# One wait in the issue order of a hybrid decoder layer: the recurrence's output products are issued two dense blocks behind the products of its states

## The chip, the cores and the metric

The kernel runs on one core of a Trainium2 chip. The metric is the device time of one execution in microseconds (us); before the change it is 469.66 us, the median of three runs (467.76 to 470.64).

## What is computed

One layer of a decoder trunk, for 512 tokens of width 1024, all in fp32. The parts that the change touches are the HGRN2 recurrence and what surrounds it; cut from the reference:

```python
xn = rmsnorm(h, norm_gain[i]).astype(dt)
proj = xn @ w_in[i]
aq, ak, av, ag, bq, bf, bi, bg, gate_a, gate_b = jnp.split(proj, split_pts, axis=-1)
...
def step(state, inp):
    qc, kc, vc, gc = inp
    cum = jnp.cumsum(gc, axis=2)
    o_inter = jnp.einsum('bhtk,bhkv->bhtv', qc * jnp.exp(cum), state)
    diff = jnp.where(causal[:, :, None], cum[:, :, :, None, :] - cum[:, :, None, :, :], LOG_DECAY_MASK)
    scores = jnp.einsum('bhtk,bhsk,bhtsk->bhts', qc, kc, jnp.exp(diff))
    o_intra = jnp.einsum('bhts,bhsv->bhtv', scores, vc)
    last = cum[:, :, -1:, :]
    state = state * jnp.exp(last[:, :, 0, :, None]) + jnp.einsum('bhsk,bhsv->bhkv', kc * jnp.exp(last - cum), vc)
    return state, o_inter + o_intra
...
yb = rmsnorm(yb, hgrn_out_gain[i].reshape(HGRN_HEADS, HGRN_VDIM)).reshape(b, s, HGRN_WIDTH)
yb = (yb * jax.nn.silu(bg.astype(f32))).astype(dt) @ w_up_b[i]
merged = jax.nn.sigmoid(gate_a.astype(f32)) * ya.astype(f32) + jax.nn.sigmoid(gate_b.astype(f32)) * yb.astype(f32)
h = h + merged.astype(dt) @ w_out[i]
```

Beside it stand a block-sparse attention with 8 heads (`ya`) and a last product with a gate (`ple`).

## The kernel before

**Dense blocks.** Every fp32 product with a weight is made of three matmuls of a rounded part and a rest (`hi*hi`, `hi*lo`, `lo*hi`). A block of one projection, 128 output columns by 512 tokens, is 24 such matmuls of 128x512 (`mm3`, L253). Its weight of 512 KB is loaded by GpSimd's queue (L227), rounded on ScalarE (`wh`, L194), and the rest is taken on VectorE (`wl`, L195); `weight` runs these two blocks ahead. The blocks stand in a fixed list, `ORDER`: for each head of the recurrence a forget block `bf` and a query block `bq`, the gates `bg` and `ag`, and the merge gates `ga` and `gb`, whose sigmoid is three instructions on ScalarE (L258 to L260).

**Side work on a planned clock.** Attention and recurrence are Python generators. Every dense matmul advances a planned clock `now` by 0.227 us (a block by 5.45 us), and a generator that yields a number is continued when the planned clock has gone on by so much. So a yielded number says how many dense blocks go in between. TensorE and SyncE keep the order in which the program issues; ScalarE's and VectorE's instructions are put in order by a scheduler that simulates the program. On each engine the order is then fixed.

**The recurrence of one head** (4 heads, h0 to h3; `hop` of h1 stands at 197 us of the profile, that of h2 at 251 us). `hgrn_intra` makes rescaled copies of keys and queries at seven sizes (`hx`, L496 to L504), and multiplies them on TensorE into two PSUM banks, `lpb` and `lpa` (L546, L551, L519): `lpb` and the first part of `lpa` beside one attention step, the rest of `lpa` (sizes 8, 4, 2) beside the next. The results are merged into `s32` (L527) and copied into the scores `sc` (L560, L563, L598). It also transposes the decayed keys through a trip to memory (L577 and four DMAs of L579, on SyncE's queue) and unpacks them on ScalarE (`hkd`, L589). `hgrn_out` multiplies keys and values into `hds` (L606), runs the states `st` through it (L610, L613), yields, and then issues seven matmuls into `hop` (L619, L621) that need `sc` and `st`. Then comes a chain that is narrow and goes to and fro: square on ScalarE (L625), transpose and sums on VectorE (L273, L275), L278 on ScalarE, L280, L264 and L265, L266 to L269, `nwide` on ScalarE (L293), transpose on VectorE (L294), and at last L627, which reads `hop` and scales it into `ho`. `hgrn_gated` multiplies by the gate (L633) and splits the result into `ybh` and `ybl`, which the blocks `ub` need.

**The banks.** `lpb`, `lpa`, `hds` and `hop` are taken in this order from two PSUM banks (tag "g"). So `lpa` of a head lies in the bank of the previous head's `hop`, and its first matmul may not start before L627 has read that `hop`.

**Attention** runs eight steps; each issues score matmuls `s` (L712), a softmax (L729 on VectorE, L731 and L733 on ScalarE) and 16 sorting DMAs on SyncE's queue (L747).

Of the kernel before, what the change touches and what calls it, by code (L numbers as in the profile page):

```python
# [57 lines left out]
def hybrid_layer_kernel(  # L58
# [29 lines left out]
    def unit(tag, name, dt=F32, shape=(128, 512)):  # L88
        return sb.tile(list(shape), dt, tag=tag, bufs=BUFS[tag], name=name)

    def bank(tag, name):
        return psum.tile([128, 512], F32, tag=tag, bufs={"mm": 3, "g": 2, "a": 3}[tag], name=name)
# [34 lines left out]
    def cost(us):  # L127
        now[0] += us
# [142 lines left out]
    def token_sums(sq, tmp, scale):  # L271

        V.transpose(tmp, sq)  # L273
        part = sb.tile([128, 16], F32, tag="n16", bufs=2, name="npart")
        V.tensor_reduce(part, tmp.rearrange("p (j c) -> p j c", c=32), axis=AX.X, op=OP.add)  # L275
        quad = sb.tile([32, 16, 4], F32, tag="n64", bufs=2, name="nquad")
        for i in range(4):
            A.activation(quad[:, :, i], part[32 * i:32 * i + 32], AF.Copy, scale=scale)  # L278
        ms = sb.tile([32, 16], F32, tag="n16", bufs=2, name="nms")
        V.tensor_reduce(ms, quad, axis=AX.X, op=OP.add)  # L280
        return ms

    def token_factor(ms):
        y = sb.tile([32, 16], F32, tag="n16b", bufs=2, name="ny")
        t = sb.tile([32, 16], F32, tag="n16b", bufs=2, name="nt")
        rsqrt(y, t, ms)
        return y

    def token_spread(dst, y):

        wide = sb.tile([128, 16], F32, tag="n16", bufs=2, name="nwide")
        for i in range(4):
            A.activation(wide[32 * i:32 * i + 32], y, AF.Copy)  # L293
        V.transpose(dst, wide[:, :, None].to_broadcast([128, 16, 32]))  # L294
# [306 lines left out]
    def hgrn_out(h, vb):  # L601
        kb, q, cum, kts = hg[h][:4]
        hv = slice(h * 128, h * 128 + 128)
        dsp = bank("g", f"hds{h}")
        for c in range(3):
            PE.matmul(dsp[:, c * 128:c * 128 + 128], kts[:, c * 128:c * 128 + 128], vb[c][:, hv],  # L606
                      start=True, stop=True)
        cost(0.65)
        st = unit("st", f"st{h}", shape=(128, 3, 128))
        V.tensor_copy(st[:, 0], dsp[:, 0:128])  # L610
        for c in (1, 2):
            e = c * 128 + 127
            V.scalar_tensor_tensor(st[:, c], st[:, c - 1], cum[:, e:e + 1], dsp[:, c * 128:c * 128 + 128],  # L613
                                   op0=OP.mult, op1=OP.add)
        yield 6.0
        op_ = bank("g", f"hop{h}")
        for c in range(NT):
            s_ = slice(c * 128, c * 128 + 128)
            PE.matmul(op_[:, s_], vb[c][:, hv], sc[:, c, :], start=True, stop=(c == 0))  # L619
            if c:  # L620
                PE.matmul(op_[:, s_], st[:, c - 1], q[:, s_], start=False, stop=True)  # L621
        cost(1.5)
        o = unit("YB", f"ho{h}")
        y = unit("N", f"hy{h}")
        A.activation(o, op_, AF.Square)  # L625
        token_spread(y, token_factor(token_sums(o, y, 1.0 / 128)))
        V.scalar_tensor_tensor(o, op_, ogain[:, h:h + 1], y, op0=OP.mult, op1=OP.mult)  # L627
        hg[h] += (o,)
# [11 lines left out]
    def hgrn_rest(h, vb, sbg, res):  # L640
        yield from hgrn_out(h, vb)
        yield from hgrn_gated(h, sbg, res)
# [400 lines left out]
```

## Time and profile before

| | us |
|---|---|
| median of three runs (lowest, highest) | 469.66 (467.76, 470.64) |
| the profiled execution | 471.74 |
| its span, first to last instruction | 470.0 |
| TensorE matmul busy | 457.8 |
| VectorE busy | 298.9 |
| ScalarE busy | 277.3 |
| mean granted TensorE clock | 0.984 |

The table of waits names for an engine which instruction it waited for: the total in us, how often, and the longest. A window row gives the busy time of each engine in a stretch, the granted TensorE clock (PEclk, 1.00 is full speed), the busy share of the DMA engines and GB/s. The chain of waits lists start, duration and piece, followed back from the last instruction. A timeline row gives start, duration, engine, line and operation, and in brackets the idle time of its engine just ahead of it and what ended that. Where two instructions follow each other without a gap, the second one's start lies some 0.1 us ahead of the first one's end.

### The profile page before, as it was taken

How to read it: one execution, taken by the hardware profiler on the slowest of the kernel's cores; microseconds unless marked ns; L12 is line 12 of the kernel's file. 1: busy time of each engine (PE TensorE's matmuls, PEld its weight loads, DVE VectorE, ACT ScalarE, POOL GpSimd, SP SyncE). 2: the span in 40 equal slices, each digit the busy share in tenths (PEclk: the TensorE clock that was granted, in tenths of full speed). 3: DMA queues.
4: the chain of work that ended last, by engine and by line, in shares of the span. 5: the costliest groups of instructions: out<-in, count | busy, mean ns of one | idle time of the engine just before them, and what ended most of it. 6: DMA issues, size and time to landing. Idle time of an engine off the chain costs nothing.

```text
span 470.0 us, 8130 instructions
## 1 busy us (share of the span) xinstructions
PE 457.8 (97%) x3094; PEld 378.8 (81%) x3094; DVE 298.9 (64%) x608; ACT 277.3 (59%) x532; POOL 38.4 (8%) x77
## 2 busy tenths in 40 slices
PE   9999999999999999699996999999999999999996
PEld 8888888788888888588885888878888788888886
DVE  5669694867698694958676572654459854553232
ACT  5758575657689886859776784965334522232201
POOL 0000100100000000000100000001111110000000
PEclk9999999999999999889997999999999999999999
DMA  8732333322323633333426153135534544223211
GB/s 249 279 98 91 111 129 107 95 87 78 102 90 93 202 96 118 106 92 130 130 68 166 54 154 117 54 84 168 176 83 133 190 147 144 100 94 111 89 46 45
DMA packets 26470, 55.30 MB, mean 118 GB/s; under 512 B 6720, under 2 KB 12608, under 8 KB 26432
## 3 DMA queue, kind: packets, MB, share of 16 engines
q0 software_dynamic: 9056, 32.51, 21.6%
q1 hardware_dynamic: 17232, 22.27, 15.4%
q8 instruction: 24, 0.39, 0.4%
q14 instruction: 14, 0.11, 0.1%
q10 hardware_dynamic: 144, 0.01, 0.0%
HBM read 46.65 MB, written 2.88 MB: 105 GB/s over the span
## 4 chain that ended last, share of the span: by engine, by line
PE 89%; DVE 4%; ACT 4%; issue 1%; DMA 1%; ACTq 0%; DVEq 0%
PE ga L253 10%; PE gb L253 10%; PE g L253 9%; PE h L253 8%; PE av L383 5%; PE bq L253 5%; PE ub L253 5%; PE bf L253 5%; PE bg L253 4%; PE bi L383 4%; PE aq L383 4%; PE ak L383 4%; PE ua L253 3%; PE pe L253 2%; PE ag L253 2%; PE s L712 2%
## 5 line engine op out<-in xcount | busy, mean ns | idle before, releaser
L194 ACT ACTIVATE wh<-wf 128x1024 fp32r<-128x1024 f32 (+1 forms) x78 | 75.5, 969 | 105.6 <-PE g L253 20.9
L195 DVE TENSOR_TENSOR wl<-wf,wh 128x1024 fp32r<-128x1024 f32 (+1 forms) x78 | 86.5, 1110 | 65.2 <-ACT wh L194 64.6
L227 POOL DMA_DIRECT2D wf<-in_w_tr_dram x30 | 15.8, 528 | 186.2 <-DVE wl L195 128.3
L253 PE MATMUL g<-hh,wh 128*128 128x512 f32 (+1 forms) x72 | 26.3, 365 | 0.0
L253 PE MATMUL g<-hl,wh 128*128 128x512 f32 (+1 forms) x72 | 26.3, 365 | 0.0
L253 PE MATMUL g<-hh,wl 128*128 128x512 f32 (+1 forms) x72 | 26.3, 365 | 0.0
L253 PE MATMUL ga<-xh,wh 128*128 128x512 f32 x64 | 26.0, 405 | 0.0
L253 PE MATMUL gb<-xh,wh 128*128 128x512 f32 x64 | 25.6, 401 | 0.0
L253 PE MATMUL ga<-xh,wl 128*128 128x512 f32 x64 | 25.4, 397 | 0.0
L253 PE MATMUL gb<-xl,wh 128*128 128x512 f32 x64 | 25.4, 397 | 0.0
L253 PE MATMUL ga<-xl,wh 128*128 128x512 f32 x64 | 25.4, 397 | 0.0
L253 PE MATMUL gb<-xh,wl 128*128 128x512 f32 x64 | 25.3, 395 | 0.0
L253 PE MATMUL h<-ml,wh 128*128 128x512 f32 x64 | 25.0, 391 | 0.2 <-DVE ml L195 0.2
L253 PE MATMUL h<-mh,wl 128*128 128x512 f32 x64 | 24.9, 390 | 0.0
L253 PE MATMUL h<-mh,wh 128*128 128x512 f32 x64 | 24.9, 389 | 0.0
L731 ACT ACTIVATE pb<-pb,ps 128x128 f32<-128x128 f32 (+3 forms) x32 | 17.6, 552 | 11.7 <-DVE ps L729 11.7
L729 DVE CUSTOM_DVE_ANT_0 pb<-s,bias 128x128 f32<-128x128 f32 (+3 forms) x28 | 12.7, 494 | 12.6 <-PE s L712 12.6
L930 DVE TENSOR_TENSOR hf<-h,xres 128x512 f32<-128x512 f32 x8 | 5.5, 691 | 18.1 <-PE h L253 18.1
L733 ACT ACTIVATE pb<-pb,ps 128x128 f32<-128x128 f32 (+3 forms) x32 | 15.9, 549 | 0.0
L498 ACT ACTIVATE hx<-hx 128x512 f32<-128x512 f32 x24 | 14.8, 623 | 1.4 <-DVE hx L497 1.3
L253 PEld LDWEIGHTS g<-hh,wl 128*128 128x128 f32 x72 | 13.6, 189 | 2.2
L253 PEld LDWEIGHTS g<-hh,wh 128*128 128x128 f32 x72 | 13.6, 189 | 2.2
(342 smaller groups left out, 1256.1 us busy)
## 6 DMA issues: line engine op xcount, KB each, us to landing
wf<-in_w_tr_dram POOLq DMA_DIRECT2D x30, 512.0 KB, 4.0
wf<-in_w_tok_dram POOLq DMA_DIRECT2D x8, 512.0 KB, 3.7
wf<-in_w_up_dram POOLq DMA_DIRECT2D x16, 256.0 KB, 2.9
wf<-in_w_o_dram POOLq DMA_DIRECT2D x8, 512.0 KB, 3.5
wf<-in_w_g_dram POOLq DMA_DIRECT2D x8, 512.0 KB, 3.6
wf<-in_w_tok_dram SPq DMA_DIRECT2D x6, 512.0 KB, 3.8
pb<-pb SPq DMA_DIRECT2D x64, 48.0 KB, 2.5
bias<-in_ed_dram SPq DMA_DIRECT2D x8, 256.0 KB, 5.4
```

Of the source, the lines that this page charges most:

```text
L194: A.activation(hi, src, AF.Copy)
L195: V.tensor_tensor(lo, src, hi.bitcast(F32), op=OP.subtract)
L227: (G if len(wraw) >= FAR else nc.sync).dma_start(raw, ap)
L253: PE.matmul(ps, a[:, k, :], b[k], start=(n == 0), stop=(n == tot - 1))
L383: PE.matmul(banks[t], a[:, s_], b[:, kk, :], start=(k == 0 and i == 0), stop=(k == KD - 1 and i == 2))
L498: A.activation(x, x, AF.Exp)
L712: PE.matmul(b_[:, o:o + nk], (qh, ql, qh)[i][js, qb * 128:qb * 128 + 128], (kh, kh, kl)[i][js, :nk], start=(i == 0), stop=(i == 2))
L729: in_order(V.tensor_tensor_reduce(p_, s_[:, so:so + nk], T[j][:, nk - 1::-1], -1.0, 3e38, OP.add, OP.min, st[:, 0:1]))
L731: A.activation(p_, p_, AF.Exp, bias=st[:, 0:1], scale=-1.0, accum_out=st[:, 1:2])
L733: A.activation(p_, p_, AF.Copy, scale=st[:, 2:3])
L930: V.tensor_tensor(t, ps, xres, op=OP.add)
```

## The change

One number: the yield in `hgrn_out` between the states' products and the output's.

```diff
@@ -612,7 +612,7 @@
             e = c * 128 + 127
             V.scalar_tensor_tensor(st[:, c], st[:, c - 1], cum[:, e:e + 1], dsp[:, c * 128:c * 128 + 128],
                                    op0=OP.mult, op1=OP.add)
-        yield 6.0
+        yield 11.0
         op_ = bank("g", f"hop{h}")
         for c in range(NT):
             s_ = slice(c * 128, c * 128 + 128)
```

No instruction is added or removed on TensorE. SyncE's order stays as it is, and GpSimd's issues stay in their places. The seven `hop` matmuls of each head go one dense block further back. In h0 they pass part of the `ak` products and a transpose, in h1 the block `gb`, in h2 and h3 a block `ga`.

TensorE in h1, before (`hop` directly behind the last matmul of `ag`):

```order
 L253 MATMUL ag_2106<-xh_487,wl_1858 128x512
-L619 MATMUL hop_2144<-sc,biv_393 128x128
-L619 MATMUL hop_2144<-sc,biv_395 128x128
-L621 MATMUL hop_2144<-ha_1376,st_2088 128x128
-L619 MATMUL hop_2144<-sc,biv_397 128x128
-L621 MATMUL hop_2144<-ha_1376,st_2088 128x128
-L619 MATMUL hop_2144<-sc,biv_399 128x128
-L621 MATMUL hop_2144<-ha_1376,st_2088 128x128
-L253 MATMUL gb_2201<-xh_414,wh_1901 128x512
```

The whole block `gb` stood behind `hop`. In the changed program `hop` follows the last matmul of `gb`:

```order
+L253 MATMUL gb_2155<-xh_487,wl_1902 128x512
+L619 MATMUL hop_2191<-sc,biv_393 128x128
+L619 MATMUL hop_2191<-sc,biv_395 128x128
+L621 MATMUL hop_2191<-ha_1376,st_2088 128x128
+L619 MATMUL hop_2191<-sc,biv_397 128x128
+L621 MATMUL hop_2191<-ha_1376,st_2088 128x128
+L619 MATMUL hop_2191<-sc,biv_399 128x128
+L621 MATMUL hop_2191<-ha_1376,st_2088 128x128
 L253 MATMUL bf_2242<-xh_414,wh_2102 128x512
```

Behind `bf` come three matmuls of `bq`, the scores `s`, `lpb` and `lpa` of the next head, in the same order as before. So one block fewer lies between `hop` and that `lpa`.

ScalarE in h1, at the chain behind `hop` (`nquad`, `nt`, `ny`, `nwide` are the chain; `hkd` the unpacked keys; `wh` rounded weights; `sgb` a sigmoid of `gb`; `ybh` the gated result):

```order
 L278 ACTIVATE nquad<-npart 32x16 x4
 L264 ACTIVATE nt<-nms,epsc 32x16
 L265 ACTIVATE ny<-nt 32x16
+L589 ACTIVATE hkd_2399<-hkt_2403 128x4x3x32
+L194 ACTIVATE wh_2269<-wf_2267 128x1024
 L293 ACTIVATE nwide<-ny 32x16 x4
-L589 ACTIVATE hkd_2399<-hkt_2403 128x4x3x32
-L194 ACTIVATE wh_2238<-wf_2236 128x1024
-L258 ACTIVATE sgb_2232<-gb_2201 128x512
-L194 ACTIVATE ybh_2186<-bg1s 128x512
```

The unpacking of the keys, which waits for their DMA, and the rounding of `wh_2269` now stand ahead of `nwide`; before, both came behind it. The rounding of `wh_2238` and the first two instructions of `sgb` moved ahead of L625 (not shown).

VectorE in h1, before, from the chain's transpose on:

```order
 L269 TENSOR_TENSOR ny<-ny,nt 32x16
-L294 STREAM_TRANSPOSE hy_2153<-nwide 128x512
-L627 SCALAR_TENSOR_TENSOR ho_2152<-hop_2144,sm,hy_2153 128x512
-L633 TENSOR_TENSOR bg1s<-bg1s,ho_2152 128x512
-L195 TENSOR_TENSOR wl_2239<-wf_2236,wh_2238 128x1024
-L195 TENSOR_TENSOR ybl_2187<-bg1s,ybh_2186 128x512
 L195 TENSOR_TENSOR wl_2270<-wf_2267,wh_2269 128x1024
```

And in the changed program, in a row:

```order
L195 TENSOR_TENSOR wl_2270<-wf_2267,wh_2269 128x1024
L294 STREAM_TRANSPOSE hy_2200<-nwide 128x512
L729 ISA pb,ps_2285<-s_2277,bias_1927 128x512
L729 ISA ps_2285 128x1
L729 ISA pb,ps_2291<-s_2278,bias_1929 128x512
L729 ISA ps_2291 128x1
L468 TENSOR_SCALAR hu_2424<-bf_2242 128x512
L496 TENSOR_TENSOR hx_8_2451<-hu_1791 128x32x8
L497 TENSOR_TENSOR hx_8_2451<-hu_1791 128x32x8
L496 TENSOR_TENSOR hx_4_2469<-hu_1791 128x64x4
L497 TENSOR_TENSOR hx_4_2469<-hu_1791 128x64x4
L627 SCALAR_TENSOR_TENSOR ho_2199<-hop_2191,sm,hy_2200 128x512
```

L627, the last reader of `hop`, now stands behind the next head's softmax on the scores `s` and four `hx` instructions. In h2 the order is the same, without L468. In h3 no `lpa` of a further head follows.

## The prediction, as put on record

> **What bounds the kernel now.** I read the page's head first, then TensorE's waits.
>
> ```profile
> span 470.0 us, 8130 instructions
> PE 457.8 (97%) x3094; PEld 378.8 (81%) x3094; DVE 298.9 (64%) x608; ACT 277.3 (59%) x532; POOL 38.4 (8%) x77
> ```
> ```profile
> PE hop L619 <- ACT sc L598: 7.1, 2, 3.6
> PE warm L161 <- PEq L1031: 0.8, 1, 0.8
> PE ak L383 <- ACT pb L663: 0.3, 1, 0.3
> PE h L253 <- DVE ml L195: 0.2, 1, 0.2
> ```
>
> TensorE is busy for 97% of the span, so what counts is what keeps it waiting. Two waits make nearly all of that: `hop` waits twice, 3.56 us each, for the scores `sc` (in h1 and h2). The windows around the two show that each costs more than its length; columns are the stretch, its length, busy time of the engines, the granted clock, DMA share and GB/s.
>
> ```profile
> 193.69:195.90 2.21, 0.00 (x0) 0.00 (x0) 2.21 (x7) 2.18 (x4) 0.14 (x1) 1.00 0.41 92
> 195.90:197.25 1.35, 0.00 (x0) 0.00 (x1) 1.35 (x4) 1.29 (x6) 0.39 (x1) 0.51 0.61 112
> 197.25:202.60 5.35, 5.35 (x20) 4.87 (x21) 2.73 (x4) 1.92 (x3) 0.53 (x1) 0.50 0.83 259
> 251.46:257.10 5.64, 5.64 (x20) 5.13 (x21) 2.82 (x4) 2.08 (x4) 0.53 (x1) 0.50 0.87 248
> ```
>
> 2.2 us into the idle stretch the granted clock falls to one half, and it stays there for 5.35 us after work has come back (5.64 us in h2). What that costs, the chain of waits tells (start, length, piece):
>
> ```profile
> 161.03 0.30 PE lpa L519 x18
> ...
> 197.25 1.22 PE hop L619 x4
> ...
> 200.60 6.55 PE gb L253 x24
> 207.15 5.44 PE bf L253 x24
> 212.59 0.68 PE bq L253 x3
> 213.27 0.90 PE s L712 x6
> ...
> 215.23 0.30 PE lpa L519 x18
> ...
> 251.46 1.22 PE hop L619 x4
> ...
> 269.61 0.30 PE lpa L519 x18
> ...
> 302.23 0.45 PE hop L619 x4
> ...
> 303.80 11.61 PE ga L253 x51
> ```
>
> At full clock a block takes 5.44, `hop` takes 303.80 - 302.23 = 1.57 (h3), and from `bq` to the first `lpa` it is 215.23 - 212.59 = 2.64. So from `hop` through two blocks to `lpa` is 1.57 + 5.44 + 5.44 + 2.64 = 15.09 us. It took 215.23 - 197.25 = 17.98 in h1 and 18.15 in h2: the slow clock costs 2.89 and 3.06. The two places together lose 7.12 + 5.95 = 13.07 us.
>
> **The change, part by part.** *The old wait goes.* `ag` of h1 ends at 193.69, and `gb` can start there: its weight was split more than ten microseconds earlier. `gb` ends at 193.69 + 5.44 = 199.13. `sc` is ready at 197.2, since its matmuls and copies stand unmoved; so `hop` doesn't wait and ends at 200.70. `bf` ends at 206.14, and 2.64 later, at **208.78**, TensorE is at the next head's `lpa`. In h2 the same sum from 247.90 gives 247.90 + 15.09 = **262.99**.
>
> *A new wait comes.* `lpa` lies in the bank of this `hop` and has to wait for L627. In the present order L627 is done at 207.8, seven us ahead of `lpa` (215.23). In the changed order one block less lies between, and L627 stands behind more. The chain up to `ny` is short enough: L625 started at 200.64 and L265 ended at 204.5.
>
> ```profile
> 204.30 0.22 ACT L265 ACTIVATE ny<-nt 32x16 f32<-32x16 f32 x1
> 205.34 0.90 ACT L293 ACTIVATE nwide<-ny 32x16 f32<-32x16 f32 x4 [0.81 <-DVE ny L269]
> 206.52 0.52 ACT L589 ACTIVATE hkd<-hkt 128x384 f32<-128x384 f32 x1 [0.28 <-DMA hkt<-hkt2there]
> 206.97 1.06 ACT L194 ACTIVATE wh<-wf 128x1024 fp32r<-128x1024 f32 x1
> 207.93 0.58 ACT L258 ACTIVATE sgb<-gb 128x512 f32<-128x512 f32 x1
> ...
> 260.46 0.52 ACT L589 ACTIVATE hkd<-hkt 128x384 f32<-128x384 f32 x1
> ```
> ```profile
> 204.37 0.58 SPq L579 DMA_DIRECT2D hkt<-hkt2there  x1
> ```
>
> Now L589 stands ahead of `nwide` on ScalarE, and L589 waits for its DMA. That DMA is the last behind 16 sorting DMAs on SyncE's queue, issued at 204.37 and used at 206.52. Neither that queue nor the transposes that feed it are moved or wait for `hop`, so 206.52 stays. Then comes `wh` at 206.97 (its buffer is free, since `bf` ends at 206.14) and `nwide` at 207.93, done 208.83. On VectorE:
>
> ```profile
> 206.26 0.71 DVE L294 STREAM_TRANSPOSE hy<-nwide 128x512 f32<-128x512 f32 x1 [0.96 <-ACT nwide L293]
> 207.08 0.75 DVE L627 SCALAR_TENSOR_TENSOR ho<-hop,sm,hy 128x512 f32<-128x512 f32 x1
> ...
> 213.50 1.23 DVE L195 TENSOR_TENSOR wl<-wf,wh 128x1024 fp32r<-128x1024 f32 x1 [3.20 <-ACT wh L194]
> 214.64 0.68 DVE L729 CUSTOM_DVE_ANT_0 pb<-s,bias 128x512 f32<-128x512 f32 x1
> ...
> 217.80 0.68 DVE L471 SCALAR_TENSOR_TENSOR ha<-bf,ha 128x512 f32<-128x512 f32 x1
> ...
> 269.01 0.68 DVE L729 CUSTOM_DVE_ANT_0 pb<-s,bias 128x512 f32<-128x512 f32 x1
> ...
> 271.58 0.15 DVE L732 RECIPROCAL ps<-ps 128x1 f32<-128x1 f32 x1
> ```
> ```profile
> 212.41 1.06 ACT L194 ACTIVATE wh<-wf 128x1024 fp32r<-128x1024 f32 x1 [1.91 <-PE bf L253]
> ```
>
> `wl` starts 213.50 - 212.41 = 1.09 behind its `wh`: 208.06. The next instruction follows 1.14 later: L294 at 209.20, and 0.62 later (0.71 less 0.09 of overlap) the softmax at 209.82; its scores have been there since 207.7. The two L729, L468 and four `hx` took 217.80 - 214.64 = 3.16: L627 starts at 212.98, ends at 213.73, and `lpa` starts at 213.78. **The new wait in h1 is 213.78 - 208.78 = 5.00 us**, against 3.56 now. In h2 from L589 at 260.46: `wh` 260.91, `wl` 262.00, L294 263.14, L729 263.76, without L468 271.58 - 269.01 = 2.57 later L627 at 266.33, `lpa` at 267.13: **4.14 us**. The two waits grow from 7.12 to 9.14 in all, by 2.02.
>
> *The slow clock* follows these idle stretches too, since both are longer than the 3.56 that brought it on. I price it as now, 2.89 and 3.06, so it adds nothing. Bounds: if the slow stretch counts from the drop (195.90 to 202.60, 6.70 us, beginning 2.2 us into the wait), a longer wait covers more of it; 6.70 - (5.00 - 2.2) = 3.9 us at half clock remain, a loss of 1.95 in place of 2.89, and likewise in h2 some 0.5 less: 1.4 saved. Upwards, 1.4 more in the same way. I take the middle.
> [...]
>
> *At nothing.* In h0 `hop` goes back behind a transpose; nobody on TensorE waits for it before `lpa` of h1 (161.03), which comes some 50 us later. In h3 L627 and the split into `ybl` come later by a block and by the softmax now ahead, some 7 us. Now:
>
> ```profile
> 313.47 0.69 DVE L195 TENSOR_TENSOR ybl<-bg3s,ybh 128x512 fp32r<-128x512 f32 x1 [0.70 <-ACT ybh L194]
> ```
>
> That is about 320.5 then. The first use is the tenth matmul of `ub`, which starts at 321.1, so at 323.2. Three us of `ga` and `ub` cover it; without that cover its lateness would be paid in full.
>
> **Sum.** 2.02 us of wait and nothing for the clock. The profiled execution took 471.74 (470.0 of span), 2.1 above the median; it would take 473.8. On the median: 469.66 + 2.02 = **471.7 us**. A change of 1% (4.7 us: below 465.0 or above 474.4) is about what a measurement of this kernel can tell from none.
>
> **Rivals.** *The stall vanishes* (A). `lpa` isn't held by the bank, or L627 comes early: all 13.07 is gained, 456.6. For it speaks that the waits name only `sc`; against it the order on VectorE, where L627 can't run ahead of a softmax whose scores come at 207.7.
>
> *The new wait is set by the scores, not by the DMA* (B). If the keys' DMA lands in time, the softmax starts at 207.77, L627 ends at 211.68, and the wait is 2.95; in h2 the scores at 261.93 give 2.36. Together 5.31 in place of 7.12: 467.9, and down to 461.9 if such waits no longer halve the clock. Against it: L589 was already waiting for that DMA, and the queue ahead of it is untouched.
>
> *The rounding of a weight is late* (C), the case that ends slower. `wh_2238` and two sigmoid steps now stand ahead of L625.
>
> ```profile
> 195.76 0.53 POOL L227 DMA_DIRECT2D wf<-in_w_tr_dram  x1 [15.54 <-DVE s L527]
> ```
> ```profile
> DMA to landing us min/median/max: 2.4/3.6/6.0
> ```
>
> The load is issued at 195.76. If it lands at t, L625 starts 2.3 later (0.96, 0.6 and 0.75 of L194, L258 and L259) and L265 ends 3.9 after that. From t = 200.3, 4.6 us behind the issue, this passes 206.52, and each further us lengthens both waits by one. At the slowest landing of any weight, 6.0, it is 1.5 each: 471.7 + 3.0 = 474.7. For it speaks the DMA share of 0.83 from 197.25 on; against it that the load has the queue to itself for the first two us.
>
> **Chances.** The forecast 0.72, A 0.03, B 0.11, C 0.14. Faster by over 1%: A and a small part of B, 0.05. Slower by over 1%: half of C and the forecast with a clock worse on both sides, 0.13. The same: 0.82. The range leaves out A, the low part of B and the end of C: from 467.5 (B with the clock as now, or the forecast with the clock's gain and a little off the waits) to 475.0 (C).
>
> **What would show it.** Right: the waits of `hop` for `sc` are gone, and in their place TensorE waits twice at `lpa` (L519) for `ho` (L627) on VectorE, some 5.0 and 4.1 us; `hop` of h1 starts about 5.4 us behind the end of `ag`; L589 starts near 206.5 and L627 of h1 near 213; the clock still falls to one half in two places. Wrong: no wait at `lpa`, or one under 3 us; L589 not ahead of `nwide` in time; a wait at `ub`; or the clock at 1.00 across the stall.

## The result: 475.76 us, slower by 1.3%

| | before | changed |
|---|---|---|
| median of 4 runs (lowest, highest), us | 469.53 (467.76, 470.64) | 475.76 (474.80, 476.15) |
| the profiled execution, us | 471.74 | 475.69 |
| its span, us | 470.0 | 473.9 |
| mean granted clock | 0.984 | 0.982 |

The ratio of the times is 1.0133, with a 95% interval of 1.0098 to 1.0168. The kernel became slower, by 1.0 to 1.7%. The forecast was 471.7 us, in a range up to 475.0.

The head of the page and TensorE's waits of the changed kernel:

```profile
span 473.9 us, 8131 instructions
PE 457.8 (97%) x3094; PEld 379.0 (80%) x3094; DVE 298.5 (63%) x608; ACT 277.0 (58%) x532; POOL 38.4 (8%) x77
```
```profile
PE lpa L519 <- DVE ho L627: 11.1, 2, 6.0
PE warm L161 <- PEq L1031: 0.8, 1, 0.8
PE ak L383 <- ACT pb L663: 0.3, 1, 0.3
PE h L253 <- DVE ml L195: 0.2, 1, 0.2
```

TensorE's busy time is the same to a tenth of a microsecond. The wait of `hop` for `sc`, 7.1 us, has gone from the list, and `lpa` waits 11.1 us for L627 in its place. 11.1 - 7.1 = 4.0, and the two profiled executions differ by 475.69 - 471.74 = 3.95. So between these two executions the waits are the whole difference. The two waits on TensorE's timeline:

```profile
215.21 0.63 PE L519 MATMUL lpa<-hx 128*32 128x16 f32 x32 [5.96 <-DVE ho L627]
...
271.20 0.63 PE L519 MATMUL lpa<-hx 128*32 128x16 f32 x32 [5.16 <-DVE ho L627]
```

Behind both, the granted clock (the third number from the end of a window row) is low again:

```profile
215.20:222.00 6.80, 6.79 (x48) 5.41 (x49) 6.80 (x19) 5.36 (x14) 0.00 (x0) 0.54 0.05 19
271.20:277.00 5.80, 5.80 (x46) 4.69 (x47) 5.80 (x17) 4.12 (x12) 0.00 (x0) 0.58 0.16 57
```

The missing share of the clock makes (1 - 0.54) x 6.80 + (1 - 0.58) x 5.80 = 5.6 us of lost time. Before the change the two stretches at half clock, 5.35 and 5.64 us in the prediction's rows, make 5.5. So the clock costs the same in these two executions.

The chain of waits shows what paced the first one:

```profile
204.92 2.88 DMA hkt<-hkt2there
...
208.34 1.05 ACT wh L194
209.41 1.22 DVE wl L195
210.64 0.62 DVE hy L294
211.26 0.57 DVE pb L729
211.85 0.60 DVE pb L729
212.46 0.60 DVE hu L468
...
214.41 0.67 DVE ho L627
215.21 0.63 PE lpa L519 x32
```

It is the chain of the prediction, link by link. Only its first link is different: the keys' DMA is under way for 2.88 us, and ScalarE waits for it. The rows of ScalarE and SyncE:

```profile
207.91 0.52 ACT L589 ACTIVATE hkd<-hkt 128x384 f32<-128x384 f32 x1 [1.36 <-DMA hkt<-hkt2there]
```
```profile
204.92 0.58 SPq L579 DMA_DIRECT2D hkt<-hkt2there  x1
```

Against before the issue is 0.55 later (204.37 to 204.92), of which 0.4 is a shift of the whole execution (the scores `s` ahead of all this start at 182.28 in place of 181.88), and L589 is 1.39 later (206.52 to 207.91). What ran beside that DMA is seen on GpSimd's queue and in the windows (last two columns: DMA share, GB/s). First the changed kernel, then the one before:

```profile
198.70 0.53 POOL L227 DMA_DIRECT2D wf<-in_w_tr_dram  x1 [2.01 <-DVE wl L195]
203.10 0.53 POOL L227 DMA_DIRECT2D wf<-in_w_tr_dram  x1 [3.87 <-DVE wl L195]
```
```profile
205.00:206.00 1.00, 1.00 (x6) 0.81 (x6) 0.21 (x1) 0.69 (x5) 0.00 (x0) 1.00 1.04 372
206.00:207.00 1.00, 1.00 (x6) 0.72 (x4) 0.35 (x3) 0.52 (x2) 0.00 (x0) 1.00 0.75 246
```
```profile
198.29 0.53 POOL L227 DMA_DIRECT2D wf<-in_w_tr_dram  x1 [2.01 <-DVE wl L195]
209.99 0.53 POOL L227 DMA_DIRECT2D wf<-in_w_tr_dram  x1 [11.17 <-DVE wl L195]
```
```profile
205.00:206.00 1.00, 1.00 (x6) 0.84 (x5) 0.27 (x2) 0.64 (x3) 0.00 (x0) 1.00 0.38 91
206.00:207.00 1.00, 1.00 (x7) 0.81 (x6) 0.71 (x1) 0.70 (x4) 0.00 (x0) 1.00 0.01 2
```

Before the change the next 512-KB weight load was issued at 209.99, when the keys had landed. Now it is issued at 203.10, ahead of the keys' DMA (204.92), and the DMA share from 205 to 207 us, while the keys are moved, is 1.04 and 0.75, against 0.38 and 0.01 before. The load waits for `wl` to free its buffer (the rows of GpSimd name L195), and that `wl` has moved. Changed, then before:

```profile
201.58 1.22 DVE L195 TENSOR_TENSOR wl<-wf,wh 128x1024 fp32r<-128x1024 f32 x1 [1.84 <-ACT wh L194]
```
```profile
208.47 1.22 DVE L195 TENSOR_TENSOR wl<-wf,wh 128x1024 fp32r<-128x1024 f32 x1
```

The rounding of that weight stands ahead of the chain now (the change's order shows it), so its buffer is free 6.9 us sooner, and the next load starts where the keys are on their way.

In h2 L589 started at 264.50 in place of 260.46. Of these 4.04 us, 3.0 is the shift of all that runs ahead of it by then (the first of the four keys' DMAs goes out at 249.41 in place of 246.41), so L589 is 1.0 late here too. About half of that is the transfer, 2.6 us in place of 2.0, behind a load issued at 259.66. The other half is the queue: its 16 sorting DMAs took 11.00 us in place of 10.43. What slowed those is not shown.

### The profile page after: what moved, and what is told of

It reads as the page before. It is cut to its first block, busy times and chain, and to the rows that moved or that the text cites. A ratio compares the mean times of both kernels' runs of the same rounds, so it can differ in the third digit from the quotient of the medians.

```text
span 473.9 us, 8131 instructions
## 1 busy us (share of the span) xinstructions
PE 457.8 (97%) x3094; PEld 379.0 (80%) x3094; DVE 298.5 (63%) x608; ACT 277.0 (58%) x532; POOL 38.4 (8%) x77
## 3 DMA queue, kind: packets, MB, share of 16 engines
HBM read 46.65 MB, written 2.88 MB: 105 GB/s over the span
## 4 chain that ended last, share of the span: by engine, by line
PE 82%; DVE 6%; ACT 3%; DMA 3%; SPq 3%; issue 1%; ACTq 0%; DVEq 0%
PE g L253 9%; PE gb L253 8%; PE h L253 8%; PE ga L253 7%; PE bq L253 5%; PE ub L253 5%; PE av L383 5%; PE bg L253 4%; PE bi L383 4%; PE aq L383 4%; PE ak L383 4%; PE bf L253 3%; PE ua L253 3%; SPq L747 3%; PE pe L253 2%; PE ag L253 2%
## 5 line engine op out<-in xcount | busy, mean ns | idle before, releaser
L195 DVE TENSOR_TENSOR wl<-wf,wh 128x1024 fp32r<-128x1024 f32 (+1 forms) x78 | 86.7, 1112 | 76.6 <-ACT wh L194 76.2
L519 PE MATMUL lpa<-hx 128*32 128x16 f32 x512 | 6.3, 189 | 11.1 <-DVE ho L627 11.1
```

The lines of the kernel that those rows point to most:

```text
L195: V.tensor_tensor(lo, src, hi.bitcast(F32), op=OP.subtract)
L519: PE.matmul(d, l[:, o:o + 32], m, start=True, stop=True)
```

## The experiments

The theory: `lpa` waits for L627 because it shares a PSUM bank with the previous `hop`; L627 is paced by ScalarE, which waits for the keys' DMA; and that DMA is late because of the weight load beside it. The rivals: the loss sits in the clock, or somewhere else along the program. Runs of the program before stand beside each group of experiments, 64 in all.

**The bank.**

```diff
-        op_ = bank("g", f"hop{h}")
+        op_ = bank("a", f"hop{h}")
```

> The changed program with hop in another PSUM bank (tag a, that of the attention's scores), so that lpa of the next head no longer has to wait for L627; the order on TensorE is that of the change. Theory (the new wait comes from the bank that lpa shares with hop, and the clock falls because TensorE stands idle there): neither hop nor lpa waits, the granted clock stays at 1.00 through h1 and h2, and the time is that of the changed program less the two waits, 11.1, and less what the slow clock costs there, 5.7: 475.7 - 16.8 = 458.9 us, 457 to 461. Rival (the time is lost elsewhere, in the later output or in loads that collide): 470 or more, with the clock still falling. Second rival (the wait only moves, to the scores s that now take turns with hop in three banks): 463 to 472 with a wait at s.

Measured: 463.30 us (463.07 to 464.38), 0.9844 of before (0.982 to 0.9867). TensorE's waits:

```profile
PE o L760 <- DMA pb<-pb: 2.2, 1, 2.2
```

None of `hop`, `lpa` and `s` stands in the list, and the clock is 1.00 from 196 to 222 us. So the bank is what made `lpa` wait; the rivals that the time is lost elsewhere, or that the wait moves to `s`, fall. The time is 4.4 us above the 458.9 expected, because a wait came that nobody had named: `o` waits 2.2 us for sorting DMAs, and the clock falls behind that.

```profile
234.30:235.13 0.83, 0.00 (x1) 0.03 (x1) 0.16 (x1) 0.83 (x4) 0.00 (x0) 0.98 0.00 0
235.13:237.00 1.87, 1.87 (x16) 1.57 (x16) 0.00 (x0) 1.87 (x6) 0.00 (x0) 0.50 0.00 0
```

The same edit in the program before:

> The program before with the same other bank for hop and nothing else. Theory (the bank matters only where hop stands late): hop still waits 3.56 us for the scores sc in h1 and h2, and the time stays within 1 us of the program before, 468.5 to 470.5. Rival (the bank's turn is worth something by itself): faster or slower by more than 2 us.

Measured: 471.18 us, 1.0006 of before (0.9984 to 1.0028), `hop` waiting 7.1 us as ever. The time is above the 470.5 expected at most, but so was the program before on that chip, 471.20. The bank by itself is worth nothing.

**The keys' DMA in ScalarE's order.**

```diff
-        A.activation(kd[:, :nk].rearrange("p (c a k) -> p a c k", c=3, a=4),
-                     kts[:, :nk].rearrange("p (a c k) -> p a c k", a=4, c=3), AF.Copy)
+        G.tensor_copy(kd[:, :nk].rearrange("p (c a k) -> p a c k", c=3, a=4),
+                      kts[:, :nk].rearrange("p (a c k) -> p a c k", a=4, c=3))
```

> The changed program with the unpacking of the keys (L589) on GpSimd in place of ScalarE, so that ScalarE does not wait for the keys' DMA ahead of wh and nwide. Theory (L627 is paced by that DMA through ScalarE's order): wh starts behind L265, 1.8 us sooner in both heads, and the waits at lpa fall from 5.96 and 5.16 to about 4.2 and 3.4; 3.6 us less, 472.1 us, 471 to 473. Rival (the softmax and its scores pace L627 on VectorE, or the unpacked keys are late for the states): the waits stay as they are, 475 to 477.

Measured: 472.16 us (470.81 to 474.17), 1.0031 of before (1.0007 to 1.0056), and the waits:

```profile
PE lpa L519 <- DVE ho L627: 8.5, 2, 4.5
```
```profile
206.22 1.06 ACT L194 ACTIVATE wh<-wf 128x1024 fp32r<-128x1024 f32 x1 [0.38 <-PE bf L253]
```

`wh` starts at 206.22 in place of 208.34, and the waits are 4.03 and 4.49 (4.2 and 3.4 were expected). In h1 the wait for the DMA is gone. What is left there, 4.03, is `wh`, `wl`, L294, the softmax and four `hx` ahead of L627. In h2 something else was late, and the chain of waits names it: a weight load of 5.23 us, and behind it `wh`, L258, L259 and L625. That is rival C of the prediction, met in an experiment.

```profile
249.54 5.23 DMA wf<-in_w_tr_dram
254.85 1.06 ACT wh L194
...
257.15 0.49 ACT ho L625
```

**The load beside it.**

```diff
+            light = len(wraw) in (36, 43)
+            if light:
+                raw, ap = raw[:, 0:1], ap[:, 0:1]
             (G if len(wraw) >= FAR else nc.sync).dma_start(raw, ap)
-            wraw.append(raw)
+            wraw.append(raw.to_broadcast([128, kn, cols]) if light else raw)
```

> The changed program with two weight loads (numbers 36 and 43, those issued at 203.10 and 259.66) cut from 512 KB to 64 KB; the blocks that use them multiply by one eighth of the weight taken eight times, so this part of the computation is left out. No instruction moves. Theory (the keys' DMA lands late because these loads now run beside it): the keys land some 2.1 us behind their issue as before the change, L589 starts 0.7 us sooner in h1 and some 0.4 in h2, and each wait at lpa shrinks by as much: 1.1 us less, 474.6 us. Rival (the DMA is late for another reason, such as the sorting DMAs ahead of it): L589 and the waits stay, 475.7 us.

Measured: 473.34 us (470.95 to 475.36), 1.0056 of before (1.0027 to 1.0086). The waits fall from 11.1 to 8.8. The runs of this kernel spread over 4.4 us, so it is the profile that decides here and not the time. Transfers issued near the keys' one, between 201 and 212 us (count, KB each, median us to landing): this kernel, then the changed one, then the one before.

```profile
wf<-in_w_tr_dram POOLq DMA_DIRECT2D x1, 64.0 KB, 2.3
hkt<-hkt2there SPq DMA_DIRECT2D x1, 48.0 KB, 2.1
```
```profile
hkt<-hkt2there SPq DMA_DIRECT2D x1, 48.0 KB, 2.9
```
```profile
hkt<-hkt2there SPq DMA_DIRECT2D x1, 48.0 KB, 2.0
```

With the load cut the keys take 2.1 us, against 2.0 before the change and 2.9 in the changed kernel. The profiles of all the kernels here say the same, each with two heads. How long the keys' DMA took, by how far ahead of it a full weight load had been issued:

| load issued ahead, us | keys' DMA, us |
|---|---|
| 0.1 to 0.9 | 4.1, 3.6, 3.8, 3.7, 3.7 |
| 1.2 to 1.6 | 3.2, 3.5, 3.6, 3.3, 3.2 |
| 1.8 to 2.2 | 2.9, 2.8, 2.6, 2.8 |
| 3.4 | 2.1 |
| more than 5 | 2.0 to 2.1 ten times, 3.0 once (its issue took 1.47 us in place of 0.58) |

In the changed kernel the load was 1.8 us ahead in h1 (203.10 to 204.92) and 2.2 in h2; before the change, the last one was 6 us ahead. The waits fell by more than the 1.1 us expected, because the sorting DMAs ahead of it also went out quicker. In h1 the 16 took 10.01 us, against 10.73 in the changed kernel and before the change. That part is not the load's: with the full loads in place it was 10.01 in the kernel with the other bank and 10.10 in a second profile of the changed kernel. In h2 the last 15 of them took 9.98 (249.00 to 258.98), against 10.45 (251.34 to 261.79); whether the load has a share in that is open.

**The clock.** First the changed program once more, for its spread:

> The changed program once more, unaltered, for the spread of its times and granted clocks beside runs of the program before. Theory (the program before pays the slow clock in some executions and not in others, because its waits of 3.56 us are only a little longer than what brings the clock down; the changed program's waits of 5 to 6 us are long enough to pay it always): runs of the program before spread over 5 us with clocks from 0.984 to 0.996, runs of the changed program over 2 us or less with clocks of 0.985 or below, near 475.5. Rival (the clock falls alike in both): the same spread and the same clocks in both, the changed program 4 us above in each.

Measured: 477.16 us (476.88 to 477.50), beside 471.2 for the program before on the same chip: 1.013 (1.0099 to 1.0161), as in the first measurement, and 1.7 us above the 475.5 expected. The granted clocks were 0.981 to 0.985. In the profile taken here the loads stood 0.9 and 1.2 us ahead of the keys' DMAs, and the waits were longer:

```profile
PE lpa L519 <- DVE ho L627: 12.5, 2, 6.6
PE bi L383 <- ACT gh L198: 1.3, 1, 1.3
```

The second line, and another 0.5 us of `bi`, belong to the first 19 us of this execution, ahead of all that the change moves; the first profile has no such wait.

The 64 runs of the program before, by their granted clock:

| clock | runs | median us | lowest to highest |
|---|---|---|---|
| 0.984 to 0.985 | 18 | 471.9 | 471.3 to 472.9 |
| 0.986 to 0.989 | 19 | 471.4 | 470.3 to 473.2 |
| 0.991 to 0.993 | 15 | 469.9 | 468.9 to 471.2 |
| 0.995 to 0.996 | 12 | 468.2 | 467.5 to 470.5 |

So the spread came as the theory had it: one and the same program pays the clock almost in full in some executions and little of it in others, while all eight runs of the changed one paid. That 3.56 us is only a little longer than what brings the clock down was the author's estimate; no run shows such a length, and in the profile before the clock fell 2.2 and 2.6 us into the two waits. What the clock is worth was measured by filling the idle time:

```diff
+        if h in (1, 2):
+            fill = bank("a", f"fill{h}")
+            for i in range(14):
+                PE.matmul(fill[:, 0:128], one, one, start=True, stop=True)
         op_ = bank("g", f"hop{h}")
```

> The program before with 14 unused 128x128 matmuls (some 3.3 us, result not read) issued ahead of hop in h1 and h2, so that TensorE works through most of the 3.56 us in which it waits for the scores; nothing of the computation is left out. Theory (the clock falls because TensorE stands idle, and that price, 5.95 us in the profiled execution, is apart from the wait): the granted clock stays at 1.00 in both places, the time falls to that of the undisturbed clock, 471.7 - 5.9 = 465.8 us in every run, 465 to 467, and the spread of the runs shrinks to about 1 us. Rival (the clock falls for another reason, or the added matmuls delay hop): no gain or a loss, 470 to 474.

Measured: 466.47 us (466.27 to 466.94), 0.9906 of before (0.9881 to 0.9932). The work fills the wait, and the clock stays up, here and behind it:

```profile
193.41 3.29 PE L619 MATMUL fill<-const-float32-1.0 128*128 128x128 f32 x28
197.14 0.71 PE L623 MATMUL hop<-sc,biv 128*128 128x128 f32 x4 [0.45 <-ACT sc L598]
```
```profile
193.30:196.60 3.30, 3.30 (x30) 3.16 (x28) 3.30 (x8) 3.25 (x7) 0.53 (x1) 1.00 0.37 85
196.60:202.00 5.40, 4.95 (x29) 4.30 (x29) 3.37 (x5) 3.29 (x9) 0.53 (x1) 1.00 0.94 263
```

The same in the changed program, 20 such matmuls ahead of the first matmul of `lpa` in h2 and h3:

> The changed program with 20 unused 128x128 matmuls (some 4.7 us, result not read) ahead of the lpa of h2 and h3, inside the new waits of 5.96 and 5.16 us; nothing of the computation is left out. Theory (of what the change costs, the waits are one part and the slow clock another): the clock stays at 1.00 and 5.7 us come back, 475.7 - 5.7 = 470 us, 469 to 471.5, while L627 and lpa stand where they stood. Compared with the filled program before, what is left is the difference of the waits alone, 4.0 us. Rival (the clock is no part of the difference): 475 or more.

Measured: 472.29 us (471.28 to 474.06), above the 471.5 expected at most, 1.0026 of before (1.0007 to 1.0045), clocks 0.996 to 1.0, and besides the fill of 4.73 each the waits were

```profile
PE lpa L519 <- DVE ho L631: 3.3, 2, 2.1
```

The idle clock costs 471.2 - 466.47 = 4.7 us in the program before and 477.16 - 472.29 = 4.9 in the changed one: about the same, though up to 1.8 of the 4.9 may be the waits of `bi`. With the clock held up in both, the difference of the programs is still 472.29 - 466.47 = 5.8, more than the 4.0 expected. In the two profiles, waits and fill make 2 x 4.73 + 3.3 = 12.8 against 2 x 3.29 + 0.9 = 7.5, which is 5.3 of it. So the rival that the loss is the clock's falls; the waits carry it.

**One head, and one block more.**

```diff
-        yield 11.0
+        yield 11.0 if h == 1 else 6.0
```

> The change in h1 alone (hop two blocks behind the states' products there, one block in the other heads). Theory: h1 loses its wait for sc, 3.56 us, and gains one at lpa of 6 to 6.6 us; h2 keeps its wait for sc of 3.56 us; the clock falls in both places as before. About half of the whole change's 6.0 us over the program before, which ran at 471.2 us in 38 runs: 474.2 us, 473 to 475.5. Rival (the loss is in one head alone, or in h0 or h3): 471 or 477.

Measured: 472.75 us (472.08 to 475.53) beside 470.28, 1.0056 (1.0028 to 1.0083); the waits are one of 6.1 us at `lpa` and one of 3.6 at `hop`. The time lies just below the numbers expected, since the program before was quicker on this chip than the 471.2 that they start from. The loss is 2.5 us, a little under half of 6: it adds up over the heads.

```diff
-        yield 11.0
+        yield 16.0
```

> One step further in the changed program's direction: hop another block later, inside the block bf (16.0 in place of 11.0). Theory (lpa waits for L627 and L627 for its chain behind hop): hop of h1 ends some 4 us later, the keys' DMA has then long landed, and the chain from the end of hop to that of L627, which takes some 10 us without a wait, sets lpa: waits of 6.5 to 8.5 us in each head, 13 to 17 in place of 11 to 12.5, with the clock at one half in both places: 477 to 483 us, 480. Rival (the wait at lpa is the keys' DMA alone): waits no longer than in the changed program, 475 to 477.

Measured: 482.11 us (480.14 to 482.69), 1.0248 (1.0194 to 1.0301), inside the numbers expected, but not by the way expected:

```profile
PE lpa L519 <- DVE ny L269: 6.1, 1, 6.1
PE lpa L519 <- DVE s L527: 6.0, 1, 6.0
PE ub L253 <- ACT ybh L194: 4.2, 1, 4.2
```
```profile
213.62 0.63 PE L519 MATMUL lpa<-hx 128*32 128x16 f32 x32 [6.11 <-DVE ny L269]
```
```profile
215.20 0.75 DVE L627 SCALAR_TENSOR_TENSOR ho<-hop,sm,hy 128x512 f32<-128x512 f32 x1
```

`lpa` starts ahead of L627 here. With `hop` so late, `lpa` was given the other of the two banks, that of its own `lpb`, and waits for L527 to read it. So this run says nothing on how L627's lateness prices the wait; it says that two banks are too few for a late `hop`, whichever of them `lpa` gets. And `ub` now waits for `ybh`, which the changed program escaped by some 3 us (its `ybl` was done at 324.3, and the first matmul that needs it started at 327.1).

**Both obstacles away.** The other bank and the keys on GpSimd, with the change:

> The changed program with hop in the attention's banks and the unpacking of the keys (L589) on GpSimd. With the other bank alone the time was 463.3 us and one wait was left: o (L760) 2.2 us for its sorting DMAs, behind a ScalarE that had waited 1.3 us for the keys' DMA, and after it the clock at 0.50. Theory (that wait too comes from L589 in ScalarE's order): ScalarE runs 1.8 us sooner, the wait at o falls below 1 us and the clock stays at 1.00: 463.3 - 1.8 - 2 = 459.5 us, 458.5 to 461. Rival (o waits for the sorting DMAs' own issue, or GpSimd delays VectorE): 463 or more.

Measured: 459.76 us (459.09 to 460.37), 0.9762 of before (0.9736 to 0.9789), with a clock of 1.0 in every run. TensorE's waits, all of them above 0.1 us:

```profile
PE warm L161 <- PEq L1031: 0.8, 1, 0.8
PE ak L383 <- ACT pb L663: 0.3, 1, 0.3
PE h L253 <- DVE ml L195: 0.2, 1, 0.2
PE o L760 <- DMA pb<-pb: 0.2, 1, 0.2
```

And the same with the change taken back:

> The program before with hop in the attention's banks and the unpacking of the keys on GpSimd, so the best kernel so far (459.8 us) with the change itself taken back. Theory (the later hop removes the wait for sc, and the other two edits only take away what it ran into): hop waits for sc again, 3.5 us twice, the clock falls in some executions, and the time is that of the program before, 471 us, 469 to 472. Rival (the two other edits gain by themselves): 460 to 468.

Measured: 471.19 us (468.51 to 473.15), 1.0013 of before (0.998 to 1.0046), `hop` waiting 7.1 us for `sc`. So the two other edits gain nothing without the later `hop`. With them it brings 11.4 us; alone it only runs into the bank.

## Why the prediction was wrong

- **The old wait goes, and TensorE comes early to `lpa`: right.** `hop` starts 5.44 us behind `ag`. TensorE reaches `lpa` at 215.21 - 5.96 = 209.25, which is 208.85 less the 0.4 of the later start; 208.78 was predicted.
- **A new wait at `lpa` for L627, through the bank: right**, shown by moving `hop` to another bank.
- **"Neither that queue nor the transposes that feed it are moved or wait for `hop`, so 206.52 stays": wrong, and this is the step that failed.** L589 started at 207.91, 1.0 later after the shift. The queue's order stood still, but a transfer on another queue came beside it. `wl` frees the buffer of the next weight load, and the prediction saw its rounding move ahead of L625 without asking what that releases. From L589 to `lpa` the working was good: 215.21 - 207.91 = 7.30 us, against 213.78 - 206.52 = 7.26. So the term "new wait", 5.00 and 4.14, was mis-sized: it measured 5.96 and 5.16. Of the 2.0 us that this is more in all, some 1.3 are the keys' transfers (2.9 and 2.6 us in place of 2.0), and some 0.7 come from the queue ahead of them, whose DMAs kept their order and went out a little slower; why is open. In the second profile of the changed program the two waits came to 12.5 together.
- **The slow clock priced as now: right,** 5.5 us before and 5.6 after in the two profiles. In the second profile of the changed program it is 4.4 (half of the times from `lpa`, at 217.35 and 273.61, to the clock's return: 222.6, where the matmuls of `bq` come every 0.23 us in place of 0.43, and, as an estimate, 277.2, since 45 matmuls of `gb` took 11.85 us there and 12.46 in the first profile, where the clock was back at 276.1), which lies within the 1.4 either way that the prediction allowed. In the first profile of the changed program the clock fell at 211.3 and came back at 221.5 in h1, and fell at 269.3 and came back at 276.1 in h2.
- **The base: too low.** The three runs shown had a median of 469.66, and 64 runs have one of 471.07. The prediction noted that the profiled execution lay 2.1 above the median, and put its sum on the median. But that sum was read from an execution that paid the clock in full (0.984), as all eight runs of the changed program did (0.981 to 0.985). From profile to profile the forecast was 473.8, and 475.69 came: 1.9 off, the two waits. The other 2.1 us of the miss of 4.1 is the base: 1.4 because those three runs were quick (469.66 against 471.07), 0.7 because the profiled execution, at a clock of 0.984, was slower than the median one.
- **Rival A was not reached by the change**, but A's time is nearly what the kernel with both obstacles removed shows, 459.76 against 456.6; that kernel has two more edits, so this is no test of A. **Rival B's floor was too low**: with the keys no longer in the way the wait in h1 was 4.03, not 2.95. B let the softmax start with its scores, at 207.77; it stands behind `wh`, `wl` and L294. **Rival C** occurred in neither profile of the changed kernel and did in one of an experiment; it had the right kind of cause, a transfer that takes longer, at the wrong transfer.
- **At nothing: right.** No wait at `ub` in the changed kernel; one block later it is there, 4.2 us.

## What to carry to other kernels

When an instruction is moved, ask of every instruction that it lets run earlier which buffer that frees and which load then starts, and look what else is on the DMA engines at that time: a queue whose order stands still is not a transfer whose time stands still (2.0 us became 2.9 here). A wait that is taken from one place can show up at the next use of the same bank (7.1 us at `hop` became 11.1 at `lpa`); here the move cost 1.3% until the bank and one DMA wait in an engine's order were taken away, and then gained 2.4%. Where the runs of one program spread with the granted clock, compare executions of like clock, and don't put a sum from one of them on the median of three.

## What the runs showed of the hardware

- The clock fell with less idle time than the waits of this kernel. It fell 2.2 and 2.6 us into the two waits of 3.56 us before the change, and 2.0 and 3.2 us into those of 5.96 and 5.16 us in the changed kernel's first profile. Behind an idle stretch of 2.16 us at `o` it was 0.50 (the kernel with the other bank); with 2.1 us left idle behind a fill it stayed at 1.00. So the moment differs, and no run shows what sets it. The low stretches, read in windows of 0.25 us, lasted 6.8 us in both heads before the change, and 10.2 and 6.8 in the changed kernel's first profile; at `o` the clock of 0.98 from 234.30 to 235.13 and of 0.75 from 237.00 to 240.00 make it 3.4.
- 3.3 us of unused matmuls in each of two waits of 3.56 us gained 4.7 us on the median, and the runs of that kernel lie within 0.7 us (4 runs) where those of the program before lie within 4.3 (13 runs).
- The last 48-KB transfer of a head's keys took 2.0 to 2.1 us, but for one of 3.0, when no full weight load had been issued in the 3 us ahead of it, and up to 4.1 when a 512-KB load from another queue had been issued just ahead of it. In the changed kernel, where it took 2.9 us in h1, the DMA share was 1.04 from 205 to 206 us, against 0.38 before.
- The copy of 128x384 (`hkd`, L589) took 0.52 us on ScalarE. On GpSimd, in two heads each of three kernels, it took 0.51 us three times, and 1.13, 1.33 and 1.59 us; those of 1.33 and 1.59 ran beside a `wl` of VectorE (L195, 128x1024, 1.23 us) and ended some 0.4 us after it.
